# A two-layer decoder trunk: light experts in two matmul passes behind a branch, with weights fetched at register addresses

## The chip, the core and the metric

The kernel runs on one core of one Trainium2 chip, in one launch. The metric is the device time of one execution in microseconds (us), lower is better. The engines are TensorE (PE, its weight loads PEld), VectorE (DVE), ScalarE (ACT), GpSimd (POOL) and SyncE (SP), which here issues the DMAs. Instructions of one engine execute in program order; engines wait for each other through semaphores.

## The reference

A trunk of two layers over 256 tokens of width 1024, float32. Layer 0 is a pooling mixer with sliding-window attention and a dense SwiGLU; layer 1 is a dilated attention with a gated convolution, and then the part that the change is about, a top-2-of-8 expert SwiGLU:

```python
D_MODEL, SEQ, N_EXPERTS, TOP_K, D_FF_EXPERT = 1024, 256, 8, 2, 3584

logits = (xt @ w_router).astype(jnp.float32)
top_logit, top_e = lax.top_k(logits, TOP_K)
gates = jax.nn.softmax(top_logit, axis=-1)
...
    def expert_block(args):
        xb, e = args
        return (jax.nn.silu(xb @ w_gate[e]) * (xb @ w_up[e])) @ w_down[e]
...
x = layer_norm(ALPHA * x + f(x))   # around every sub-layer
```

256 tokens with two experts each are 512 pairs over 8 experts, 64 on average. The weights of the experts are 8 x 3 x 1024 x 3584 float32 numbers.

## The kernel before, in words

**Products in three passes.** Every float32 operand is split into a rounded high part and the low remainder (`split`: ACT casts the high part, DVE subtracts it). A product is then three matmuls into the same PSUM bank (`mm3`, lines 253 to 256): high x high, low x high, high x low. In the experts the tokens are the stationary operand (128 x 128) and the weights are the moving one (128 x 512).

**The weight stream.** All weights lie in DRAM as one stream of pieces of 128 x 2048 floats (1 MB), in the order in which they are used. `Weights` loads them into raw slots with two DMAs each (line 157, issued by SP), `hi` casts the high part (line 200, ACT, tile wh, 4 buffers), `lo` makes the low part (line 216, DVE, tile wl, 3 buffers) and frees the raw slot, and the next load goes into it. `take` hands a piece to the matmuls and `drop` frees its wh and wl and pumps the pieces that follow: wh may be up to three pieces ahead of use and wl up to two. The order of the work is that of the program (a manual schedule).

**The experts.** The router finds for each token and expert a slot in the expert's list (`slot`). The first 128 tokens of an expert are gathered by one-hot matmuls (`Gather`, lines 1094 to 1126), for two experts at a time, 128 columns each, during the last two chunks of the expert before; the gathered high and low parts (xh, xl) have a tile each. An expert is done in 7 chunks of 512 inner columns (loop at line 1213), 6 pieces each. A chunk takes two pieces of gate, two of up (`half_proj`, 16 x 3 = 48 matmuls), then the two pieces of down of the chunk before (`down_half`, 8 x 3 = 24 matmuls). Between them stand Silu on ACT (line 1218), the product on DVE (line 1225), four transposes of h on PE (`flip_h`, line 1136) and the split of the transposed h (lines 127, 128). After an expert's last chunk its output is split and added to the tokens through one-hot matmuls and the gate (`combine`, lines 1165 to 1168).

**The end.** The last chunk's down product is merged in parts. A register with the largest count is then loaded on every engine (line 1305), and a branch (line 1307) enters a loop over all experts only where an expert has more than 128 tokens. That loop addresses its weights by a register. The last layer norm and the stores follow.

Of the kernel before, what the change touches and what calls it, by code (L numbers as in the profile page):

```python
# [37 lines left out]
KEEP, FINE = (8, 20, 16), 10  # L38

C_ID, C_RANK, C_INV, C_END = 0, 128, 136, 168  # L40
# [4 lines left out]
def f32_consts():  # L45
    c = np.zeros((128, C_END), np.float32)
    c[:, C_ID:C_RANK] = np.eye(128)
    c[:, C_INV:C_END] = np.float32(10000.0) ** (-np.arange(32, dtype=np.float32) / np.float32(32))
    c[:, C_RANK:C_INV] = 8 - np.arange(8)
    return c  # L50
# [36 lines left out]
def trunk(ctx, tc, stream, x_tok, x_t, pos, ln_w, ln_b, pool_bd, pool_sc, sinks, conv_w, router, cf, cb, windows,  # L87
# [6 lines left out]
    wsp = ctx.enter_context(tc.tile_pool(name="wsp", bufs=AHEAD + 1))  # L94
    wlp = ctx.enter_context(tc.tile_pool(name="wlp", bufs=AHEAD))
    raw1 = ctx.enter_context(tc.tile_pool(name="raw1", bufs=RAW1))
# [11 lines left out]
    def bank():  # L108
        return ps1.tile([128, 512], F32, name="bank")
# [4 lines left out]
    def acc():  # L114
        return ps2.tile([128, 512], F32, name="acc")
# [13 lines left out]

    class Weights:  # L130
        def __init__(self):
            self.order = list(range(MOE_BASE + 4))
            for s in range(1, NE * NCH):
                self.order += [MOE_BASE + 6 * s + j for j in range(6)]
            self.order += [MOE_BASE + 6 * NE * NCH + j for j in (4, 5)]
            self.raw, self.split, self.owner = {}, {}, {}
            self.free = {(raw1, "raw"): RAW1}
# [5 lines left out]
        def slot(self, dt=F32, last=False):  # L143
            pool = [p for p in self.free if self.free[p]][-1 if last else 0]
            self.free[pool] -= 1
            return pool, pool[0].tile([128, PIECE], dt, name="raw", tag=pool[1])

        def load(self):
            k = len(self.owner)
            self.owner[k], self.raw[k] = self.slot()  # L150
            self.fetch(k, range(2))

        def fetch(self, k, parts, of=2):
            w = PIECE // of
            for q in parts:
                c = slice(q * w, (q + 1) * w)
                nc.sync.dma_start(self.raw[k][:, c], stream[self.order[k]][:, c])

        def top_up(self):
            while len(self.owner) < len(self.order) and sum(self.free.values()) > self.held:  # L160
                self.load()

        def lend(self, tag):
            self.free[big, tag] = 1
            self.top_up()
# [5 lines left out]
        def borrow(self):  # L171
            self.held -= 1
            return self.slot(F32R, True)

        def give_back(self, pool):
            self.free[pool] += 1
            self.top_up()
# [15 lines left out]
        def hi(self, ahead=AHEAD):  # L193
# [3 lines left out]
            if q == 0:  # L197
                self.split[k] = [wsp.tile([128, PIECE], F32R, name="wh"), None]
# [5 lines left out]
        def lo(self):  # L204
# [3 lines left out]
            if q == 0:  # L208
                if k == MOE_BASE - 1:
                    wl = big_tile("xth")  # L210
                else:
                    wl = (ep if k < OUT_BASE and k % 4 == 3 else wlp).tile([128, PIECE], F32R, name="wl")
# [5 lines left out]
            if self.at_lo[0] > k:  # L218
                self.raw.pop(k)
                self.give_back(self.owner[k])  # L220
# [45 lines left out]
    iota = consts.tile([128, B_MASK - B_IOTA], BF16, name="iota")  # L266
# [4 lines left out]
    posi = small.tile([128, 2], I32, name="posi")  # L271
    psc = small.tile([128, 2], F32, name="psc")
# [194 lines left out]
    with tc.tile_pool(name="tmpp", bufs=1, side="right") as tmpp:  # L467
# [13 lines left out]
        for k in range(2):  # L481
            W.owner[k], W.raw[k] = W.slot()
# [481 lines left out]
    raw2 = ctx.enter_context(tc.tile_pool(name="raw2", bufs=RAW2, side="right"))  # L964
# [10 lines left out]
    raw3 = ctx.enter_context(tc.tile_pool(name="raw3", bufs=RAW3))  # L975
    W.free[raw2, "raw"], W.free[raw3, "raw"] = RAW2, RAW3
    W.hold(2)
    mm, na, nb, oa, ob = proj_out(wb, lambda: None)
    ctx.enter_context(tc.manual_schedule())
    held = [W.borrow() for _ in range(2)]  # L980
    xkh, xkl = [t.rearrange("p (i d) -> p i d", i=2) for _, t in held]
# [76 lines left out]
    rank = cst[:, None, C_RANK:C_INV].to_broadcast([128, 2, NE])  # L1058
# [34 lines left out]
    class Gather:  # L1093
        def __init__(self, pool, e0, n, base, tiles):
            self.n, w = n, n * 128
            self.w = w
            self.pool = pool
            self.oh = pool.tile([128, 2, n, 128], F32R, name="oh", bufs=1)
            for i in range(2):
                for e in range(n):  # L1100
                    nc.vector.tensor_scalar(self.oh[:, i, e], iota, slot[:, i, ds(e0 + e, 1)], -float(base),
                                            op0=OP.subtract, op1=OP.is_equal)
            self.xg = [t.rearrange("p (k s) -> p k s", s=w) for t in tiles]

        def half(self, c, a, b, copy):
            w, per = self.w, 512 // self.w
            src = (xkh, xkl)[a]
            for k in range(per):
                for i in range(2):
                    nc.tensor.matmul(b[:, k * w:(k + 1) * w], src[:, i, (c + k) * 128:(c + k + 1) * 128],  # L1110
                                     self.oh[:, i].rearrange("p e s -> p (e s)"), start=i == 0, stop=i == 1)
            copy(self.xg[a][:, c:c + per], b.rearrange("p (k s) -> p k s", s=w))

        def part(self, c):
            self.half(c, 0, bank(), nc.scalar.copy)
            self.half(c, 1, bank(), nc.vector.tensor_copy)

        def back(self):
            n = self.n
            b = bank()  # L1120
            for e in range(n):
                for i in range(2):
                    c = e * 2 + i
                    nc.tensor.transpose(b[:, c * 128:(c + 1) * 128], self.oh[:, i, e].bitcast(F32), identf)
            self.oht = self.pool.tile([128, n, 2, 128], F32R, name="oht", bufs=1)
            nc.scalar.copy(self.oht, b[:, :n * 256].rearrange("p (e i t) -> p e i t", e=n, i=2))
# [6 lines left out]
    def flip_h(pool, h):  # L1133
# [3 lines left out]
        hh = pool.tile([128, 4, 128], F32R, name="hh")  # L1137
        hl = pool.tile([128, 4, 128], F32R, name="hl")
# [3 lines left out]
    def down_half(y, ht, j, n, p):  # L1142
# [26 lines left out]

    ln2.close()  # L1170
    moe = ctx.enter_context(ExitStack())
    m2 = moe.enter_context(tc.tile_pool(name="mo2", bufs=2, side="right"))
    ga = Gather(m2, 0, 2, 0, [big_tile(t) for t in ("mh", "ml")])
    nc.vector.tensor_sub(xkl[:, 1], x[:, 1], xkh[:, 1].bitcast(F32))
    W.lo()
    for c in range(0, KC, 2):
        ga.half(c, 0, acc(), nc.scalar.copy)
    for c in range(0, KC, 2):
        ga.half(c, 1, bank(), nc.vector.tensor_copy if c % 4 == 0 else nc.scalar.copy)
# [3 lines left out]
    most = rt.tile([128, 1], F32, name="most")  # L1183
    nc.vector.tensor_reduce(most, psb[:, 16:24], axis=AX.X, op=OP.max)
    mosti = rt.tile([128, 1], I32, name="mosti")
    nc.vector.tensor_copy(mosti, most)
    gate = small3("gate")

# [8 lines left out]

    def spread(a, h):
# [5 lines left out]
    lent = []  # L1204
    gathers = {0: ga}
    prev = todo = None
    for e, n in [(e, n) for e in range(NE) for n in range(NCH)]:
        xh, xl = [t[:, :, tok(e % 2)] for t in gathers[e // 2].xg]
        gu = []
        for a in range(2):  # L1210
            b = bank()
            for j in range(2):
# [238 lines left out]
```

## Time and profile before

| | |
|---|---|
| time, median of 3 runs | 1467.49 us (1467.12 to 1468.24) |
| span of the profiled execution | 1466.0 us |
| PE busy / weight loads | 1438.0 us (98%) / 1219.7 us (83%) |
| DVE busy | 1174.3 us (80%) |
| ACT busy | 952.1 us (65%) |
| mean granted TensorE clock | 0.995 |
| read from HBM | 424.88 MB, 291 GB/s over the span |
| wl, line 216 (DVE) | 474 instructions, 907.9 us |
| wh, line 200 (ACT) | 476 instructions, 772.1 us |

The span runs from the first to the last instruction of the profiled execution; its time as a run is not given beside it, and the median of the runs is 1.5 us above the span. In the slices of the profile a digit is the busy share in tenths. A row of a group gives the line, the engine, the operation, the tiles (out<-in), the shapes and the count, then busy time and the mean of one, then the idle time before it and what ended it. Matmul durations overlap (their ends are modelled), so the price of one is read from the distance of two starts.

### The profile page before, as it was taken

The page shows a single profiled execution, that of the slowest core. Times are in us where ns is not written, and L with a number is a line of the kernel's source. Part 1 is how long each engine was busy: PE and PEld are TensorE (multiplying, and loading weights), DVE is VectorE, ACT ScalarE, POOL GpSimd, SP SyncE. Part 2 cuts the span into 40 slices and gives each one's busy share as a digit, 9 for nine tenths or more (in the row PEclk, how much of TensorE's full clock was granted, in tenths as well). Part 3 has the DMA queues.
Part 4 walks back from the last instruction along what each step waited for, and adds up shares of the span by engine and source line. Part 5 has one row for each costly group of instructions (what it writes and reads, how often), then busy time and mean ns, then how long its engine had stood idle before and what let it go on. Part 6 is the DMA issues. An engine that isn't in the chain of part 4 may idle for free. (4 is left out here: it accounts for less than half of the span.)

```text
span 1466.0 us, 20100 instructions
## 1 busy us (share of the span) xinstructions
PE 1438.0 (98%) x7665; PEld 1219.7 (83%) x7665; DVE 1174.3 (80%) x1069; ACT 952.1 (65%) x921; POOL 2.5 (0%) x8
## 2 busy tenths in 40 slices
PE   8999999999999999999999999999999999999995
PEld 6889999889997788888888888888888888778884
DVE  6766454686658898988888899898888889889887
ACT  5735444455446777777777777777777777777773
POOL 0000000000000000000000000000000000000000
PEclk9999999999999999999999999999999999999998
DMA  8627655454257999999999999999999899999980
GB/s 260 213 83 233 201 174 190 156 184 162 66 189 299 365 344 363 374 338 311 348 384 355 364 377 346 337 372 410 362 365 341 307 341 369 352 339 340 395 306 31
DMA packets 119323, 426.71 MB, mean 291 GB/s; under 512 B 14130, under 2 KB 14898, under 8 KB 119220
## 3 DMA queue, kind: packets, MB, share of 16 engines
q1 hardware_dynamic: 118356, 424.34, 79.9%
q0 software_dynamic: 576, 0.62, 0.3%
q8 instruction: 62, 1.02, 0.3%
q10 hardware_dynamic: 288, 0.39, 0.1%
q14 instruction: 41, 0.34, 0.1%
HBM read 424.88 MB, written 1.05 MB: 291 GB/s over the span
## 5 line engine op out<-in xcount | busy, mean ns | idle before, releaser
L216 DVE TENSOR_TENSOR wl<-raw,wh 128x2048 fp32r<-128x2048 f32 (+2 forms) x474 | 907.9, 1940 | 97.0 <-ACT wh L200 58.5
L200 ACT CAST wh<-raw 128x2048 fp32r<-128x2048 f32 (+2 forms) x476 | 772.1, 1631 | 159.0 <-PE bank L255 65.2
L254 PE MATMUL acc<-wh,hh 128*128 128x512 f32 (+1 forms) x564 | 221.1, 392 | 0.0
L255 PE MATMUL acc<-wh,hl 128*128 128x512 f32 (+1 forms) x564 | 215.8, 383 | 0.0
L256 PE MATMUL acc<-wl,hh 128*128 128x512 f32 (+1 forms) x564 | 215.6, 382 | 0.0
L254 PE MATMUL bank<-wh,raw 128*128 128x512 f32 x448 | 174.7, 390 | 0.6 <-DVE x L1168 0.6
L254 PE MATMUL bank<-wh,mh 128*128 128x512 f32 x448 | 174.6, 390 | 0.0
L256 PE MATMUL bank<-wl,mh 128*128 128x512 f32 x448 | 174.6, 390 | 0.0
L256 PE MATMUL bank<-wl,raw 128*128 128x512 f32 x448 | 174.6, 390 | 0.0
L255 PE MATMUL bank<-wh,ml 128*128 128x512 f32 x448 | 174.4, 389 | 0.0
L255 PE MATMUL bank<-wh,raw 128*128 128x512 f32 x448 | 174.3, 389 | 0.0
L254 PEld LDWEIGHTS acc<-wh,hh 128*128 128x128 f32 x564 | 105.9, 188 | 22.4 <-issue 3.0
L256 PEld LDWEIGHTS acc<-wl,hh 128*128 128x128 f32 x564 | 105.8, 188 | 22.4
L255 PEld LDWEIGHTS acc<-wh,hl 128*128 128x128 f32 x564 | 106.1, 188 | 19.8 <-DVE hl L128 0.3
L254 PE MATMUL bank<-xth,wh 128*128 128x256 f32 x416 | 118.1, 284 | 0.0
L256 PE MATMUL bank<-xtl,wh 128*128 128x256 f32 x416 | 117.6, 283 | 0.0
L255 PE MATMUL bank<-xth,wl 128*128 128x256 f32 x416 | 117.2, 282 | 0.0
L254 PEld LDWEIGHTS bank<-wh,raw 128*128 128x128 f32 x448 | 84.1, 188 | 18.9 <-DVE x L1168 1.7
L254 PEld LDWEIGHTS bank<-wh,mh 128*128 128x128 f32 x448 | 84.1, 188 | 18.0 <-DVE x L1168 0.6
L256 PEld LDWEIGHTS bank<-wl,raw 128*128 128x128 f32 x448 | 84.1, 188 | 17.7
L256 PEld LDWEIGHTS bank<-wl,mh 128*128 128x128 f32 x448 | 84.1, 188 | 17.6
L255 PEld LDWEIGHTS bank<-wh,ml 128*128 128x128 f32 x448 | 84.1, 188 | 17.3
(246 smaller groups left out, 1668.6 us busy)
## 6 DMA issues: line engine op xcount, KB each, us to landing
raw<-in_stream SPq DMA_DIRECT2D x794, 512.0 KB, 6.7
ln_wb<-in_ln_w SPq DMA_DIRECT2D x3, 512.0 KB, 6.7
ln_wb<-in_ln_b SPq DMA_DIRECT2D x3, 512.0 KB, 10.0
xraw<-in_x_t SPq DMA_DIRECT2D x4, 256.0 KB, 7.4
raw<-in_stream SPq DMA_DIRECT2D x4, 256.0 KB, 6.4
x<-in_x_tok SPq DMA_DIRECT2D x1, 1024.0 KB
win<-in_windows SPq DMA_DIRECT2D x1, 768.0 KB, 11.4
out_dram<-x SPq DMA_DIRECT2D x2, 256.0 KB, 2.0
```

Source lines behind the costliest of these rows:

```text
L200: nc.scalar.copy(self.split[k][0][:, c], self.raw[k][:, c])
L216: nc.vector.tensor_sub(wl[:, c], self.raw[k][:, c], wh[:, c].bitcast(F32))
L254: nc.tensor.matmul(o, ah, bh, start=start, stop=False)
L255: nc.tensor.matmul(o, al, bh, start=False, stop=False)
L256: nc.tensor.matmul(o, ah, bl, start=False, stop=stop)
```

## The change

1. **Sorting on the chip.** After the first chunk of expert 0 the experts 1 to 7 are sorted by their counts on DVE (`sort_experts`). Each engine loads into registers the number of experts 1 to 7 with at most 64 tokens (`nlight`) and the largest count (`nmost`); SP also loads seven addresses into the weight stream.
2. **A branch with two arms.** After the fourth chunk of expert 0, `nlight >= 5` selects an arm. In the first the experts at places 1 to 5 of the sorted order are light and expert 0 and the last two are wide (three passes as before); in the second all are wide. Both contain the rest of the experts and the tail.
3. **Light experts.** The gathered tile has 64 columns of high parts and 64 of low parts side by side as one stationary operand, and a product is two matmuls (with wh and with wl). Rows 0 to 63 and 64 to 127 of the result are added by matmuls with a folding matrix, which also transpose it. The product and the split of h are on 256 columns instead of 512, and Silu too; gate and up are first copied out of PSUM by ACT.
4. **Gathers.** Units are [0], [1, 2], [3, 4], [5], [6], [7] in the first arm, each gathered in 32 matmuls of 128 columns during the last two chunks of the unit before.
5. **Buffers.** Rotating pools become named tiles that are used in turn (`Rings`), so that both arms find them at the same place. Three raw slots become fixed (the tokens' parts and y); the experts' gathers no longer borrow slots.
6. **Smaller moves.** `gates` from the fourth chunk to the first; the load of `nmost` from the end to the third chunk.

```diff
+LIGHT, NLIGHT = 64, 5
+    c[:, C_FOLD:C_INV] = np.arange(128)[:, None] % LIGHT == np.arange(LIGHT)
...
+        def place(self, k, c):
+            if k < MOE_BASE + 4:
+                return stream[self.order[k]][:, c]
+            p, n, j = self.order[k]
+            at = MOE_BASE + 6 * (n + (j >= 4)) + j
+            return stream[ds(self.base[p] + at, 1), :, c] if p else stream[at][:, c]
...
+    W.give_back(*[raw3.tile([128, PIECE], F32, name=f"raw{RAW1 + i}") for i in range(RAW2 + RAW3 - 3)])
...
+    def half_light(b, p, j, xg):
+        for k in range(4):
+            kk = 4 * j + k
+            nc.tensor.matmul(b, xg[:, kk], p[0][:, k], start=kk == 0, stop=False)
+            nc.tensor.matmul(b, xg[:, kk], p[1][:, k], start=False, stop=kk == KC - 1)
+
+    def flip_light(g, u):
+        b = bank()
+        for a, src in enumerate((g, u)):
+            for k in range(4):
+                c = (a * 4 + k) * LIGHT
+                nc.tensor.matmul(b[:, c:c + LIGHT], src[:, k * 128:(k + 1) * 128], fold, start=True, stop=True)
+        h = g[:, :4 * LIGHT]
+        nc.scalar.activation(h, b[:, :4 * LIGHT], AF.Silu)
+        ht = rings.next("hh")
+        s3 = h.rearrange("p (k t) -> p k t", t=LIGHT)
+
+        def rest():
+            nc.vector.tensor_mul(h, h, b[:, 4 * LIGHT:])
+            nc.scalar.copy(ht[:, :, :LIGHT], s3)
+
+        def low():
+            nc.vector.tensor_sub(ht[:, :, LIGHT:], s3, ht[:, :, :LIGHT].bitcast(F32))
+        return (ht,), rest, low
...
-                mm3(o, ht[0][:, c], ht[1][:, c], ph[:, c], pl[:, c], n == 0 and c == 0, n == NCH - 1 and c == 3)
+                start, stop = n == 0 and c == 0, n == NCH - 1 and c == 3
+                if len(ht) == 2:
+                    mm3(o, ht[0][:, c], ht[1][:, c], ph[:, c], pl[:, c], start, stop)
+                else:
+                    nc.tensor.matmul(o, ht[0][:, c], ph[:, c], start=start, stop=False)
+                    nc.tensor.matmul(o, ht[0][:, c], pl[:, c], start=False, stop=stop)
...
+        nc.vector.tensor_scalar(idx, rank, -1.0, 8.0, op0=OP.mult, op1=OP.add)
+        nc.vector.scalar_tensor_tensor(key, cnt, 8.0, idx, op0=OP.mult, op1=OP.add)
+        nc.vector.memset(key[:, 0:1], -1.0)
+        nc.vector.tensor_tensor(grid, cols(key), rows(key), op=OP.is_lt)
+        nc.vector.tensor_reduce(pos, grid, axis=AX.X, op=OP.add)
...
+        nc.vector.tensor_scalar(key[:, 1:], cnt[:, 1:], float(LIGHT), None, op0=OP.is_le)
+        nc.vector.tensor_reduce(outs[:, NE:NE + 1], key[:, 1:], axis=AX.X, op=OP.add)
...
+    for n in range(NCH - 3):
+        first.step(0, n)
+        if n == 0:
+            gates()
+            sort_experts()
+        if n == 2:
+            W.base = [0, *nc.values_load_multi_w_load_instructions(
+                ints[0:1, 1:NE], engines=[mybir.EngineType.SP], min_val=0, max_val=(NE - 1) * PER_EXPERT)[1]]
+            nlight = nc.values_load(ints[0:1, NE:NE + 1], min_val=0, max_val=NE - 1)
+            nmost = nc.values_load(ints[0:1, NE + 1:NE + 2], min_val=0, max_val=T)
+    arms = [[[0], [1, 2], [3, 4], [5], [6], [7]], [[e] for e in range(NE)]]
+    state = W.state()
+    ends = []
+    with tc.If(nlight >= NLIGHT) as cmp:
+        arm = first.copy(arms[0], arms[0][1:4])
+        for s in range(NCH - 3, NE * NCH):
+            arm.step(*divmod(s, NCH))
+        ends.append(tail(arm))
+    W.restore(state)
+    with cmp.Else():
+        arm = first.copy(arms[1], [])
+        for s in range(NCH - 3, NE * NCH):
+            arm.step(*divmod(s, NCH))
+        ends.append(tail(arm))
```

The order of the work in one chunk of a light expert (`Experts.step`): gate's two pieces; the copy of gate (ACT); up's two pieces; the copy of up; the first down piece of the chunk before; the fold (PE) and Silu (ACT); the second down piece; the product (DVE) and the high part of h (ACT). The low part of h (DVE) follows after the next chunk's first piece. In the chunk n == 2 of a light expert its one-hot is built again on DVE (`back`) and transposed on PE.

More of the change, by code (lines that the diff above doesn't have):

```diff
@@ L141, in __init__ @@
             self.at_hi = self.at_lo = (0, 0)
[L143 to L146, printed above, removed]
         def load(self):
-            k = len(self.owner)
-            self.owner[k], self.raw[k] = self.slot()
+            k = self.loaded
+            self.loaded += 1
+            self.raw[k] = self.free.pop(0)
             self.fetch(k, range(2))
@@ L481, in trunk @@
         for k in range(2):
-            W.owner[k], W.raw[k] = W.slot()
+            W.raw[k] = W.free.pop(0)
+        W.loaded = 2
         load_x(0)
@@ L1091, in trunk, with __init__ @@
     nc.vector.tensor_add(slot, off, psb[:, :16].rearrange("p (i e) -> p i e", e=NE))
[L1093 to L1098, printed above, removed]
+    class Unit:
+        def __init__(self, tile, first, n, slots, base=0):
+            self.first, self.n, self.slots, self.base = first, n, slots, base
+            self.wide = n == 0
+            n = max(n, 1)
+            self.oh = rings.next("oh")
+            w = 128 if self.wide else LIGHT
@@ L1112, in half @@
[L1112 to L1119, printed above, removed]
-            b = bank()
[L1121 to L1126, printed above, removed]
+                    nc.tensor.matmul(b[:, k * 128:(k + 1) * 128], src[:, i, (c + k) * 128:(c + k + 1) * 128],
+                                     self.oh[:, i], start=i == 0, stop=i == 1)
@@ L1182, in trunk @@
     W.lo()
[L1183 to L1186, printed above, removed]
     gate = small3("gate")
+    fold = cst[:, C_FOLD:C_INV]
+    slots, gate_of = hots[0], small3("gates")
+    ints = rt.tile([128, NE + 2], I32, name="ints")
     def gates():
@@ L1291, in trunk @@
-    finish(down_half(y, ht, 0, n, W.take(None)))
-    W.drop()
-    split(yh[:, :512], yl[:, :512], y[0])
-    last = down_half(y, ht, 1, n, W.take(None))
-    parts = [slice(512, 768), slice(768, D)]
-    next(last)
-    merge(0, 512)
-    split(yh[:, parts[0]], yl[:, parts[0]], y[1][:, :256])
-    next(last)
-    split(yh[:, parts[1]], yl[:, parts[1]], y[2][:, :256])
-    warm(AF.Sqrt, ht[0][:, 0].bitcast(F32))
-    for m in parts:
-        merge(m.start, 256)
-    nmost = nc.values_load(mosti[0:1, 0:1], min_val=0, max_val=T)
@@ L1314, in trunk @@
+    st, wb = ends[-1]
+    with tc.If(nmost > 128):
+        rings.add("raw", W.free[:2])
+        with tc.For_i(0, NE, 1) as e:
+            ga = Unit(places[1], e, 0, slot, 128)
+            for j in range(4):
+                ga.part(j)
+            ga.back(e)
             y = acc2()
             def get(w, at):
-                raw = raw2.tile([128, PIECE], F32, name="raw", tag="raw")
-                wh = wsp.tile([128, PIECE], F32R, name="wh")
-                wl = wlp.tile([128, PIECE], F32R, name="wl")
+                raw, wh, wl = rings.next("raw"), rings.next("wh"), rings.next("wl")
```

386 lines of the change are left out of this document (241 added, 145 removed).

## The prediction

> **What bounds the kernel now.** I read the page's 40 slices first, then a table of stretches, then the costliest groups between 700 and 1300 us by shape, then the timeline of one chunk of one expert, and last the waits of the DMA queue. In the slices the experts begin in the 13th or 14th, where PE goes to 9 for good and the DMA engines go to 9 with it.
>
> ```profile
> PE   8999999999999999999999999999999999999995
> DVE  6766454686658898988888899898888889889887
> ACT  5735444455446777777777777777777777777773
> DMA  8627655454257999999999999999999899999980
> GB/s 260 213 83 233 201 174 190 156 184 162 66 189 299 365 344 363 374 338 311 348 384 355 364 377 346 337 372 410 362 365 341 307 341 369 352 339 340 395 306 31
> 600.00:620.00 20.00, 20.00 (x91) 16.27 (x90) 19.47 (x14) 13.51 (x10) 0.00 (x0) 1.00 1.00 365
> 980.00:1020.00 40.00, 40.00 (x184) 32.90 (x184) 34.79 (x21) 28.88 (x21) 0.00 (x0) 1.00 1.03 410
> 480.00:600.00 120.00, 120.00 (x543) 98.71 (x542) 105.53 (x65) 91.52 (x62) 0.00 (x0) 1.00 0.99 361
> 723.00:845.00 122.00, 122.00 (x552) 100.20 (x551) 107.56 (x64) 88.68 (x60) 0.00 (x0) 1.00 0.97 363
> ```
>
> The last four rows are stretches: length, then busy time of PE, PEld, DVE, ACT, POOL, then granted clock, DMA share and GB/s. PE is busy without a gap at a full clock: TensorE is the bound. But two others are close. DVE has 107.56 of 122 us (88%), and the DMA engines are in use 97% of the time at 363 GB/s. A third less matmul is therefore not a third less time. The question is how far the period of a chunk can fall before DVE, ACT or the DMA takes over.
>
> ```profile
> L216 DVE TENSOR_TENSOR wl<-raw,wh 128x2048 fp32r<-128x2048 f32 x205 | 462.7, 2286 | 19.9 <-PE bank L256 18.7 <-DMA raw<-in_stream 1.2
> L200 ACT CAST wh<-raw 128x2048 fp32r<-128x2048 f32 x205 | 392.1, 1913 | 63.5 <-PE bank L255 43.3 <-issue 11.3 <-PE acc L255 4.4
> L1225 DVE TENSOR_TENSOR h<-h,bank 128x512 f32<-128x512 f32 x35 | 24.0, 685 | 9.4 <-PE bank L256 9.4
> L127 ACT CAST hh<-bank 128x512 fp32r<-128x512 f32 x34 | 20.0, 588 | 48.4 <-PE bank L1136 48.4
> L1168 DVE SCALAR_TENSOR_TENSOR x<-bank,gate,x 128x512 f32<-128x512 f32 x20 | 13.6, 739 | 0.0
> L788 DVE TENSOR_TENSOR sg<-sg,bank 128x256 f32<-128x256 f32 x20 | 8.4, 421 | 40.7 <-ACT sg L787 40.7
> L787 ACT ACTIVATE sg<-bank 128x256 f32<-128x256 f32 x20 | 7.7, 384 | 59.0 <-PE bank L256 59.0
> L1225 DVE TENSOR_TENSOR h<-h,bank x56: 669/687/690, 478.3 to 1436.3; 128x512 f32<-128x512 f32 x56
> ```
>
> Each chunk (512 of an expert's 3584 inner columns) takes six 1 MB pieces, and each piece costs DVE 2.286 us (wl) and ACT 1.913 us (wh), whatever PE does with it. The last row gives the period: 56 chunks, 958.0 us from the first to the last, 17.42 on average, 121.9 us per expert of seven.
>
> ```profile
> 890.79 0.69 DVE L1225 TENSOR_TENSOR h<-h,bank 128x512 f32<-128x512 f32 x1 [0.38 <-PE bank L256]
> 895.25 6.69 DVE L216 TENSOR_TENSOR wl<-raw,wh 128x2048 fp32r<-128x2048 f32 x3
> 907.69 0.69 DVE L1225 TENSOR_TENSOR h<-h,bank 128x512 f32<-128x512 f32 x1 [0.38 <-PE bank L256]
> 900.00 0.39 PE L254 MATMUL bank<-wh,raw 128*128 128x512 f32 x1
> 902.04 0.39 PE L254 MATMUL bank<-wh,raw 128*128 128x512 f32 x1
> 910.29 0.60 PE L1136 MATMUL bank<-cst,h 128*128 128x128 f32 x4
> 918.94 1.11 PE L1110 MATMUL bank<-oh,raw 128*128 128x256 f32 x8
> 396.48 0.78 PE L947 MATMUL bank<-v,pt 128*128 128x64 f32 x6
> 397.07 0.36 PE L919 MATMUL bank<-kth,qt 128*128 128x256 f32 x1
> L947 PE MATMUL bank<-v,pt 128*128 128x64 f32 x144 | 18.6, 268 | 0.0
> ```
>
> A bare chunk is 907.69 - 890.79 = 16.9 us. Nine matmuls lie between 900.00 and 902.04, so one 512-column matmul costs 0.227 us, and 72 of them with four transposes (0.6) make the 16.9.
>
> **The light chunk.** The input decides first whether it is run. The reference's own router on its inputs gives the experts 72, 72, 59, 63, 55, 73, 57 and 61 tokens. Five of experts 1 to 7 have at most 64, which is just NLIGHT, so experts 1 to 5 of the sorted order run light and three (expert 0 and the last two) stay wide.
>
> PE: 48 matmuls instead of 72 are 10.9 us. The four transposes become eight plain f32 matmuls of 64 columns (fold). L947 has the same shapes: 8 x (3 + 6) = 72 in the code and 144 in the trace, so each is recorded twice, and six records take 397.07 - 396.48 = 0.59 us. Sixteen records are 1.6 us. Together 12.5 us, 4.4 less.
>
> DVE: six wl back to back are 6 x 2.23 = 13.4 us (6.69 for three). The product and the low part of h shrink from 128x512 (0.69) to 128x256 (0.42). Together 14.2 us. Per expert, with the combine (4 x 0.68 = 2.7), the split of y (1.4) and one-hots and gather copies (about 1.2), 7 x 14.2 + 5.3 = 105 us.
>
> ACT: six wh are 11.5; two new evictions of 128x512 before the fold 1.2; Silu and high part on 256 columns 0.8. Together 13.5, and per expert about 97 us.
>
> DMA: 6 x 1.0486 = 6.29 MB. The stretch 980 to 1020 shows 410 GB/s held for 40 us: 15.3 us per chunk, 107.4 per expert. The 361 to 365 of the other stretches is what PE asked for. DVE's wl takes 2.287 us in that stretch (the row below), as elsewhere.
>
> ```profile
> L216 DVE TENSOR_TENSOR wl<-raw,wh 128x2048 fp32r<-128x2048 f32 x15 | 34.0, 2287 | 1.6 <-PE bank L256 1.6
> ACT wh L200 <- PE bank L255: 43.3, 55, 0.8
> ```
>
> So PE falls from first to last, and DVE (105) and the DMA (107.4) are next. The DMA has a credit: up to 11 raw slots, say 8 of them full when the light experts begin, are 8 x 2.56 = 20 us over the five, which makes its share 103. DVE is then the bound at no more than the 97% that it reaches in the stretch 600 to 620 (19.47 of 20). ACT, which executes in order, has 13.5 us of work beside DVE's 14.2, so 0.7 us per chunk is all that it may lose in waiting for PE ahead of the two evictions and Silu. The code lets wh run three pieces ahead of use and wl two, which covers a wait of about one piece. That slack is thin, so I take 96%: 105 / 0.96 = 109 us per light expert. Ends: 105 (DVE with no gap) and 118 (a bare chunk of today, no gain but in what is around it).
>
> A light expert in the middle of today's run costs 7 x 16.9 = 118.3, plus 2.2 for combine and back, 120.5. Five of them: 5 x (120.5 - 109) = **57 us gained**.
>
> **The gathers.** Today three pair gathers stand on PE's path, each four parts of 8 matmuls or 4 x 1.11 = 4.5 us. Afterwards there are five, of which those in expert 0 and in the seventh fall in wide, PE-bound chunks (9 us); the other three lie under DVE in light chunks. **4.5 us gained.**
>
> **What is added.** Rows for the serial parts:
>
> ```profile
> 460.07 0.17 DVE L1070 TENSOR_TENSOR hot<-eq,best 128x16 f32<-128x16 f32 x1
> L1305 DVEq TENSOR_LOAD <-mosti x1: 542/542/542, 1453.0 to 1453.0; - x1
> L1307 DVEq COMPARE_BRANCH  x1: 72/72/72, 1453.7 to 1453.7; - x1
> L1307 PEldq COMPARE_BRANCH  x1: 3892/3892/3892, 1451.2 to 1451.2; - x1
> 1456.63 0.38 DVE ln_mv L365 x2
> L157 SPq DMA_DIRECT2D raw<-in_stream x798: 327/424/1627, 1.2 to 1418.3; - x200
> SPq L157 <- DVE wl L216: 574.4, 250, 9.6
> ```
>
> Sorting is about 21 DVE operations of 0.2 us, with the six of gates moved from the fourth chunk to the first: 5 us ahead of the wl of the second chunk, where DVE is just catching up with PE. Its idle share covers some; I take 2 (0 to 5). Two register loads on each engine, 0.54 us each, in the third chunk: 1 (0 to 1). SP loads nine values; behind it wait only DMA issues, with some 8 pieces (over 20 us of PE's work) loaded ahead: 0, and 4 if the slots were empty. The branch into the first arm should fall through (0.07 us for the compare itself): 1, between 0 and the 5 of an emptied lookahead. At the end each engine jumps over the other arm and then over the overflow loop. Today's one taken branch costs DVE 1456.63 - 1453.7 = 2.9 us before the last norm; a second costs 2.9 more, and the load of nmost (0.54) leaves this place: 2.3 (0.9 to 3.9, the last from PE's row). The copy of cnt, the 32 KB of fold and one raw slot fewer in the out-projection: 1 together. Persistent buffers carry the same dependences as the rotating ones: 0, or 3 either way from a few finer or coarser waits. SP: twelve issues per chunk at 0.424 are 5.1 of 16.9 us, and it mostly waits for DVE; a register address adds register work to each, and 0.5 more would still be hidden. Sum of the added: **7 us lost** (2 to 18).
>
> The Trainium skill's "Runtime: NRT & Kernel Launch", Instruction fetch mechanics, says that a taken branch out of the fetched window stalls for a DMA fetch; the 2.9 us above agree, and no row here tells what a fall-through costs.
>
> **Sum.** 57 + 4.5 - 7 = 54.5 us off the profiled span of 1466.0: 1411.5. The runs' median is 1467.49, 1.5 above that span: **1413**.
>
> **Rivals.**
>
> *The DMA is full already.* For it: a share of 0.97 to 1.00 at 361 to 365 GB/s in most stretches. If 361 is the ceiling, a chunk takes 6.29 / 0.361 = 17.4 us with or without the third pass, nothing is gained, and with the added 7 the time is 1474; at 385 it is 114 per expert before the credit, 110 after it, and the forecast hardly moves. Against it: 410 at a share of 1.03. Chance 0.11, in between more likely than the end: 1440 to 1474.
>
> The Trainium skill's "HBM Reference", Specifications (TRN2), gives an effective 358 GB/s per core, by which a chunk could not go under 17.6 us and the change would gain nothing; it adds that a core streaming alone measures more, about 425. The 40 us at 410 bear out the second, as an estimate 14.8 us per chunk, under DVE's 15.
>
> *ACT and DVE hold each other up.* ACT needs 13.5 of the chunk's 15 and stands in order behind PE twice more than today. If each of the two evictions and Silu costs the 0.8 us of idle that ACT shows before wh today (43.3 us in 55 waits), the thin slack is gone and a chunk takes 16 to 16.5: 1430 to 1450. Chance 0.10.
>
> *The light arm isn't run.* 63 and 61 are near 64, and with one light expert fewer all experts take three passes: seven gathers instead of three (18 us), 7 added, and a taken branch at the start (2.9): 1495, slower. Against it: the counts. Chance 0.05.
>
> *SP becomes the bound: slower.* Place: the twelve register-addressed issues of each chunk after the first four. It decides when one issue costs over 16.9 / 12 = 1.41 us. At the longest of today's issues, 1.63, a chunk takes 19.5 us and 52 chunks lose 2.6 each: about 1600. Against it: 0.424 is the median, and the register work would have to cost twice that again. Chance 0.05.
>
> **How the numbers follow.** Forecast 0.69 (1390 to 1435 by itself), ACT rival 0.10, DMA 0.11, light arm not run 0.05, SP 0.05. Lower end: light experts at 105 with 2 added, 1388. Upper end: into the ACT and DMA rivals, 1450. A change under 0.2% (3 us) can't be told from none here. Faster: 0.69 + 0.10 + 0.08 of the DMA's = 0.87. Same 0.02. Slower: 0.05 + 0.05 + 0.01 = 0.11.
>
> **What would show it.** In the changed profile's five light experts: a period near 15.6 us, DVE at 95% or more, PE near 0.85, 400 GB/s or so, wl still near 2.29 us; L947's doubling seen again in the fold; in the three wide experts 16.9 as before; two taken branches before the last norm. It is wrong if the rate stays at 365 while raw slots stand empty (DMA rival), if ACT's waits for PE in the light stretch are long and DVE's share is under 90% (ACT rival), if SP never waits for DVE, or if 72 matmuls a chunk are still there.

## The result, and the profile after

The changed kernel takes **1399.64 us** (median of 4, 1398.26 to 1401.76) against 1467.75 us for the kernel before beside it: a ratio of 0.954, interval 0.9525 to 0.9552. The forecast was 1413 us with a range of 1388 to 1450; the time lies inside it, 13 us under the point. The profiled execution has a span of 1399.8 us.

Two of the slices' rows of the page after (VectorE's busy tenths, then GB/s):

```profile
DVE  6766555496665889799999999999999998889875
GB/s 259 237 55 222 207 182 193 186 122 209 134 91 232 253 327 362 346 367 399 409 408 409 408 409 409 408 409 408 408 409 404 409 409 404 408 391 261 361 239 34
```

From the 18th slice DVE stands at 9, and from the 20th the DMA engines move 404 to 409 GB/s for 16 slices on end, some 560 us. Stretches (length, then busy time of PE, PEld, DVE, ACT, POOL, then granted clock, DMA share, GB/s): the first two lie in light experts, the third in the wide experts at the end.

```profile
720.00:830.00 110.00, 103.40 (x507) 83.89 (x507) 108.41 (x76) 93.91 (x81) 0.00 (x0) 0.98 1.03 409
830.00:940.00 110.00, 102.46 (x489) 82.49 (x488) 106.62 (x67) 92.97 (x78) 0.00 (x0) 0.97 1.03 409
1134.00:1250.00 116.00, 114.87 (x535) 94.86 (x534) 101.77 (x64) 85.30 (x60) 0.00 (x0) 1.00 1.02 405
```

In the light experts DVE is busy for 97 to 99% of the time. The rows of 600 to 1130 us by shape, for wl and the fold, and the row of the product h on DVE:

```profile
L254 DVE TENSOR_TENSOR wl<-raw,wh 128x2048 fp32r<-128x2048 f32 x211 | 473.1, 2283 | 16.3 <-ACT wh L238 9.7 <-issue 3.6 <-DMA raw<-in_stream 2.7
L1192 PE MATMUL bank<-cst,h 128*128 128x64 f32 x280 | 35.6, 271 | 0.0
```

```profile
L1199 DVE TENSOR_TENSOR h<-h,bank x35: 404/410/423, 609.7 to 1124.6; 128x256 f32<-128x256 f32 x35
```

A wl still costs 2.283 us, and DVE was idle ahead of it for 16 us in 530. The row of h is the period: 35 light chunks, 514.9 us from the first product to the last, 15.14 on average, 106.0 per expert of seven. The waits of SP in 600 to 1130 us (total, times, longest):

```profile
SPq L179 <- DMA raw<-in_stream: 261.2, 349, 1.6
SPq L179 <- DVE wl L254: 37.3, 40, 3.7
```

SP waited almost always for an earlier transfer to land and seldom for DVE to free a slot. One light chunk on DVE's timeline:

```profile
671.51 0.41 DVE L1199 TENSOR_TENSOR h<-h,bank 128x256 f32<-128x256 f32 x1
671.84 2.28 DVE L254 TENSOR_TENSOR wl<-raw,wh 128x2048 fp32r<-128x2048 f32 x1
674.04 0.41 DVE L1203 TENSOR_TENSOR hh<-h,hh 128x256 fp32r<-128x256 f32 x1
674.38 11.09 DVE L254 TENSOR_TENSOR wl<-raw,wh 128x2048 fp32r<-128x2048 f32 x5
685.39 0.41 DVE L1199 TENSOR_TENSOR h<-h,bank 128x256 f32<-128x256 f32 x1
```

685.39 - 671.51 = 13.88 us with nothing between the instructions: six wl and the two halves of h. Three such bare chunks on end, as a stretch:

```profile
657.63:699.27 41.64, 40.11 (x193) 31.69 (x192) 41.64 (x26) 37.88 (x30) 0.00 (x0) 1.00 1.03 410
```

DVE is busy for all of it, and the DMA engines are full as well.

Where the 66.2 us of the span went, from products (`h<-h,bank`) that both kernels have. The row of them all in before stands in the prediction (478.3 to 1436.3); two single ones of before, from DVE's timeline:

```profile
575.61 0.69 DVE L1225 TENSOR_TENSOR h<-h,bank 128x512 f32<-128x512 f32 x1 [0.38 <-PE bank L256]
1207.14 0.69 DVE L1225 TENSOR_TENSOR h<-h,bank 128x512 f32<-128x512 f32 x1 [0.38 <-PE bank L256]
```

And of after, the row of all wide ones, and two from the timeline:

```profile
L1370 DVE TENSOR_TENSOR h<-h,bank x21: 669/687/689, 482.8 to 1365.5; 128x512 f32<-128x512 f32 x21
```

```profile
588.59 0.68 DVE L1370 TENSOR_TENSOR h<-h,bank 128x512 f32<-128x512 f32 x1
1134.67 0.68 DVE L1370 TENSOR_TENSOR h<-h,bank 128x512 f32<-128x512 f32 x1
```

| stretch | before | after | difference | forecast's terms for it |
|---|---|---|---|---|
| start to expert 0's first product | 478.3 | 482.8 | +4.5 | 0 (persistent buffers), small things 1 |
| expert 0, first to seventh product | 97.3 | 105.8 | +8.5 | sort 2, loads 1, branch 1, a gather 4.5 |
| to the first product of the seventh expert (five light ones) | 631.5 | 546.1 | -85.4 | light experts -57, three gathers -13.5 |
| the last two experts | 229.2 | 230.8 | +1.7 | a gather 4.5 |
| last product to the end | 29.7 | 34.3 | +4.6 | two jumps 2.3 |
| sum | 1466.0 | 1399.8 | -66.2 | -54.5 (rounded terms) |

In the light experts the gain was 15 us larger than forecast, and the start, the sort and the end cost more than forecast. The first row is one execution against one: in the ten profiles of this case whose kernels share the changed one's code up to the experts, the first product lands between 480.1 and 484.8 us (median 482.8).

### The profile page after: what moved, and what is told of

Read it like the earlier page. It is cut to its first block, busy times and chain, and to the rows that moved or that the text cites. A ratio compares the mean times of both kernels' runs of the same rounds, so it can differ in the third digit from the quotient of the medians.

```text
span 1399.8 us, 20835 instructions
## 1 busy us (share of the span) xinstructions
PE 1329.3 (95%) x7309; PEld 1124.5 (80%) x7309; DVE 1147.9 (82%) x1093; ACT 963.9 (69%) x1001; POOL 2.5 (0%) x8
## 5 line engine op out<-in xcount | busy, mean ns | idle before, releaser
L1185 PE MATMUL bank<-wl,ml 128*128 128x512 f32 x336 | 133.6, 398 | 4.0 <-DVE wl L254 4.0
L1228 PE MATMUL acc<-wh,hh 128*128 128x512 f32 x280 | 116.9, 417 | 0.0
L1229 PE MATMUL acc<-wl,hh 128*128 128x512 f32 x280 | 115.1, 411 | 1.6 <-DVE wl L254 0.4
L291 PE MATMUL acc<-wh,hh 128*128 128x512 f32 (+1 forms) x284 | 107.7, 380 | 0.0
L292 PE MATMUL acc<-wh,hl 128*128 128x512 f32 (+1 forms) x284 | 105.0, 370 | 0.6 <-DVE hl L130 0.6
L293 PE MATMUL acc<-wl,hh 128*128 128x512 f32 (+1 forms) x284 | 105.0, 370 | 0.0
L1184 PE MATMUL bank<-wh,mh 128*128 128x512 f32 x224 | 89.7, 401 | 0.3
L291 PE MATMUL bank<-wh,mh 128*128 128x512 f32 x224 | 88.3, 394 | 0.8 <-DVE x L1245 0.8
L292 PE MATMUL bank<-wh,mh 128*128 128x512 f32 x224 | 87.8, 392 | 0.0
L291 PEld LDWEIGHTS bank<-xth,wh 128*128 128x128 f32 x416 | 79.8, 192 | 0.4
L292 PEld LDWEIGHTS bank<-xth,wl 128*128 128x128 f32 x416 | 79.8, 192 | 0.4
L293 PEld LDWEIGHTS bank<-xtl,wh 128*128 128x128 f32 x416 | 79.8, 192 | 0.0
## 6 DMA issues: line engine op xcount, KB each, us to landing
raw<-in_stream SPq DMA_DIRECT2D x794, 512.0 KB, 10.1
```

The lines of the kernel that those rows point to most:

```text
L291: nc.tensor.matmul(o, ah, bh, start=start, stop=False)
L292: nc.tensor.matmul(o, al, bh, start=False, stop=False)
L293: nc.tensor.matmul(o, ah, bl, start=False, stop=stop)
L1184: nc.tensor.matmul(b, xg[:, kk], p[0][:, k], start=kk == 0, stop=False)
L1185: nc.tensor.matmul(b, xg[:, kk], p[1][:, k], start=False, stop=kk == KC - 1)
L1228: nc.tensor.matmul(o, ht[0][:, c], ph[:, c], start=start, stop=False)
```

## Experiments: what sets the light expert

**A third pass again.** In light experts the matmul with wl is issued twice, in `half_light` and in `down_half`.

```diff
             nc.tensor.matmul(b, xg[:, kk], p[0][:, k], start=kk == 0, stop=False)
+            nc.tensor.matmul(b, xg[:, kk], p[1][:, k], start=False, stop=False)
             nc.tensor.matmul(b, xg[:, kk], p[1][:, k], start=False, stop=kk == KC - 1)
```

> In the light experts each product with wl is issued twice, so that a chunk has 72 matmuls again beside the fold (the low part counts double in the output). Theory (the third pass was what bound the chunk): PE needs 72 x 0.227 + 1.6 = 17.9 us per chunk, a light expert takes about 129 us instead of 105, and the time is about 1520 us. Rival (the gain came from the buffers, the order of the experts or earlier loads, and the pass was hidden anyway): within 10 us of 1400.

Measured: **1532.15 us** in one run, 132.5 more than the changed kernel. Two products of neighbouring chunks and a stretch of its light experts:

```profile
949.25 0.42 DVE L1200 TENSOR_TENSOR h<-h,bank 128x256 f32<-128x256 f32 x1
967.40 0.42 DVE L1200 TENSOR_TENSOR h<-h,bank 128x256 f32<-128x256 f32 x1
```

```profile
720.00:830.00 110.00, 110.00 (x539) 92.36 (x538) 88.75 (x59) 76.70 (x64) 0.00 (x0) 1.00 0.94 341
```

PE is the bound again, and a bare chunk takes 18.15 us, more than the 16.9 of a wide one; the fold, at 1.6 us dearer than the transposes at 0.6, is most of the difference. Without the 24 extra matmuls (0.227 each) the light chunk would be 12.7 us of PE. The gain of the change is thus the skipped pass, and a bare chunk stopped at 13.88 instead of 12.7.

**All experts wide.** The light arm needs eight light experts of seven and is never entered. The expectation below says that the branch stays; the trace says otherwise. The branch's line, 1462, has two instructions on each of five engines in the changed kernel's trace and none on any engine here. The register is declared to hold at most seven, so the condition was probably settled when the kernel was built; that is not shown. So this run has neither the entry nor a jump over the other arm.

```diff
-LIGHT, NLIGHT = 64, 5
+LIGHT, NLIGHT = 64, 8
```

> NLIGHT is 8, so the branch takes the second arm and every expert has three passes; sorting, register addresses, persistent buffers and the branch stay. Theory (these parts only cost): the time before plus four more gathers (18 us) plus what the trace of the changed kernel shows as lost at the start (4.5), at the sort (4.8) and at the end (4.6), plus a taken branch (3): about 1503 us. Rival (the buffers or the addresses give part of the gain): 1470 us or less.

Measured: **1487.9 us** in one run, span 1486.1, 20.1 above the span before; between forecast and rival. The products run from 484.7 to 1456.0:

```profile
L1370 DVE TENSOR_TENSOR h<-h,bank x56: 667/687/689, 484.7 to 1456.0; 128x512 f32<-128x512 f32 x56
```

So 6.4 us lie ahead of the first product, 13.3 between the first and the last, 0.4 behind. Of the 13.3 the sort takes 4.8 (below). The 8.5 left are put down to seven gathers one by one in place of three for two, about half of the 18 that the forecast's rival took; they were not timed singly. The end costs nothing here, where one jump stands ahead of the last norm as before the change. The light arm, with its branch and its second jump, is worth 88 us.

**VectorE or the DMA freed, and then both.** In light experts the low parts are made for half of the columns; or half of each piece is loaded; or both. The matmuls read the other half from what the buffers held. Each kernel ran once.

```diff
+    def of_light(at):
+        return isinstance(at, tuple) and 1 <= at[0] <= 5
...
-            self.fetch(k, range(2))
+            self.fetch(k, range(1 if of_light(self.order[k]) else 2))
...
+            if of_light(self.order[k]):
+                c = slice(0, PIECE // 2)
```

> In the light experts DVE makes wl for half of each piece's columns only (the other half keeps older numbers). Theory (DVE binds the light chunk, and the DMA at its 409 GB/s stands just behind it): the DMA then binds, 210 pieces x 2.564 us less some 8 that are loaded ahead are 518 us against 523 now, so 1393 to 1400 us. Rival A (DVE alone binds, the DMA has room): down to ACT's 97 us per expert, about 1362 us. Rival B (ACT and PE hold each other up): no change, 1400 us.

> In the light experts only half of each piece is loaded (the other half keeps older numbers); DVE, ACT and PE do all their work. Theory (DVE binds): DVE has its 103 to 104 us per expert still, so 1393 to 1400 us, with the DMA share near a half in this stretch. Rival A of the run before (DVE alone): the same. Rival C (the DMA binds and DVE only waits for it): DVE's share of the stretch falls well under 97% now and the time falls by more than 10 us.

> In the five light experts half of each weight piece is loaded and the low parts are made for half of the columns (the matmuls read the rest from what the buffers held before). Freeing VectorE alone gave 0 us and freeing the DMA engines alone 5 us. Theory (the two tie, each keeps the time when the other is freed): with both freed the next limit is TensorE, whose light chunk was reckoned at 12.5 us and was seen at 12.7 us while the DMA engines still had loaded buffers in hand; so the light experts fall from 104.7 to about 100 to 102 us each, and the time to 1374 to 1388 us. Rival (the engines hold each other up through the order of the work, whatever the load): no better than the DMA-freed kernel, 1392 us or more. A second rival: VectorE and the DMA engines alone set it, and TensorE is far from its limit: below 1365 us.

Measured: half the low parts **1399.52 us**, half the loads **1394.36 us**, both **1361.12 us**. One stretch and the period of each, in this order (and two neighbouring products of the last):

```profile
720.00:830.00 110.00, 101.21 (x500) 83.59 (x499) 63.12 (x73) 94.79 (x81) 0.00 (x0) 0.98 1.03 409
```

```profile
L1204 DVE TENSOR_TENSOR h<-h,bank x35: 410/414/423, 609.1 to 1121.2; 128x256 f32<-128x256 f32 x35
```

```profile
720.00:830.00 110.00, 103.55 (x501) 84.11 (x500) 106.91 (x72) 93.08 (x81) 0.00 (x0) 0.97 0.61 203
```

```profile
L1202 DVE TENSOR_TENSOR h<-h,bank x35: 407/413/421, 607.3 to 1118.0; 128x256 f32<-128x256 f32 x35
```

```profile
720.00:830.00 110.00, 106.26 (x532) 89.18 (x531) 68.72 (x78) 100.55 (x89) 0.00 (x0) 0.98 0.69 222
```

```profile
L1204 DVE TENSOR_TENSOR h<-h,bank x35: 410/416/423, 611.0 to 1083.1; 128x256 f32<-128x256 f32 x35
```

```profile
746.33 0.41 DVE L1204 TENSOR_TENSOR h<-h,bank 128x256 f32<-128x256 f32 x1
759.05 0.41 DVE L1204 TENSOR_TENSOR h<-h,bank 128x256 f32<-128x256 f32 x1
```

With DVE at 57% the 35 chunks still take 512.1 us (514.9 before the edit; 513.8 to 515.3 in the profiles of the six other kernels here that leave the light chunk as it is), now at the 409 GB/s of the DMA. With the DMA at 61% they take 510.7, now on DVE alone (97%). With both freed they take 472.1. The two limits stand within 1% of each other, and either one alone keeps the time. The 409 GB/s move 34 chunks of 6.29 MB in 523 us; 512 is possible because loaded slots were drained meanwhile. The kernel with half the low parts shows it: three bare chunks of its first light expert, then three of its third:

```profile
649.85:688.00 38.15, 38.15 (x194) 32.41 (x192) 24.06 (x26) 37.44 (x31) 0.00 (x0) 1.00 1.03 409
855.04:901.73 46.69, 42.36 (x194) 34.80 (x193) 24.06 (x26) 38.97 (x31) 0.00 (x0) 0.93 1.03 409
```

The first three take 12.7 us each, from slots that were full; the later three take 15.4 to 16.0, and 6.29 MB at 409 GB/s are 15.4. With both freed a bare chunk takes 759.05 - 746.33 = 12.72 us, the same as PE's 12.7 worked out from the third pass. Three of them there:

```profile
651.76:689.89 38.13, 38.13 (x193) 32.40 (x192) 24.07 (x26) 37.42 (x31) 0.00 (x0) 1.00 0.74 247
```

TensorE is the next limit, 1.2 us below today's bare chunk. ScalarE is busy for 37.42 of the same 38.13 us (98%), so it stands right behind: fewer matmuls alone could take at most 0.2 us more off a bare chunk. The expectation's theory had the mechanism, but its 100 to 102 us per expert were reckoned badly: seven chunks of 12.7 are 89, and with combine and gathers 97 was measured. The second rival named the right time for the wrong reason, since PE is busy without a gap in the bare chunks there. That the engines hold each other up through their order is refuted: the same order of work goes through 43 us faster.

## Experiments: what the change added

**The persistent buffers alone.** The kernel before, with wh, wl and the single raw slots as named tiles in turn, and nothing else.

```diff
-    wsp = ctx.enter_context(tc.tile_pool(name="wsp", bufs=AHEAD + 1))
+    wsp = ctx.enter_context(tc.tile_pool(name="wsp", bufs=1))
...
-                self.split[k] = [wsp.tile([128, PIECE], F32R, name="wh"), None]
+                self.split[k] = [turn_of("wh"), None]
```

> The kernel before, with only one part of the change: the high-part, low-part and single raw weight buffers are made once and handed out in turn, in place of pools that rotate. The three passes, the order of the experts and the end stay as before. Theory (the 4.5 us by which the first expert starts later after the change come from the persistent buffers): the first expert's first product lands 4 to 6 us later than 478.3 us, and the time is 1471 to 1474 us. Rival (the delay is from another part of the change): within 0.2% of before, 1467 to 1469 us, with the first product at 478 us.

Measured: **1471.61 us** against 1468.78 (medians of 10 and 13), ratio 1.0019 (1.0008 to 1.0031), 2.8 us more. The first product lands at 482.8 us as after the change, and from there to the last product it is 958.0 us as before:

```profile
L1237 DVE TENSOR_TENSOR h<-h,bank x56: 669/687/690, 482.8 to 1440.8; 128x512 f32<-128x512 f32 x56
```

The largest single step is near 322 us in layer 1. PE's one wait between 310 and 335 us in the kernel before, and ACT's weight casts between the first copy of v (at 315.13 us) and the cast that PE waits for:

```profile
PE bank L320 <- ACT kth L322: 0.4, 1, 0.4
```

```profile
317.13 1.05 ACT L200 CAST wh<-raw 128x1024 fp32r<-128x1024 f32 x1 [1.75 <-DMA raw<-in_stream]
318.33 1.05 ACT L200 CAST wh<-raw 128x1024 fp32r<-128x1024 f32 x1
320.76 1.05 ACT L200 CAST wh<-raw 128x1024 fp32r<-128x1024 f32 x1 [1.38 <-DMA raw<-in_stream]
321.73 0.36 ACT L322 CAST kth<-bank 128x256 fp32r<-128x256 f32 x1
```

The same with persistent buffers (the copy of v is at 316.05):

```profile
PE bank L332 <- ACT kth L334: 2.4, 1, 2.4
```

```profile
318.23 1.05 ACT L212 CAST wh<-raw 128x1024 fp32r<-128x1024 f32 x1 [1.91 <-DMA raw<-in_stream]
320.05 1.05 ACT L212 CAST wh<-raw 128x1024 fp32r<-128x1024 f32 x1 [0.77 <-DMA raw<-in_stream]
322.45 1.05 ACT L212 CAST wh<-raw 128x1024 fp32r<-128x1024 f32 x1 [1.15 <-PE bank L318]
324.05 1.04 ACT L212 CAST wh<-raw 128x1024 fp32r<-128x1024 f32 x1 [0.56 <-DMA raw<-in_stream]
325.00 0.36 ACT L334 CAST kth<-bank 128x256 fp32r<-128x256 f32 x1
```

The dependences are the same, but in this attention the order of ACT's instructions is not written out by hand, and with other buffers it came out otherwise: four weight casts in place of three stand ahead of the key's cast (kth), three of them wait for their transfers, and the key waits behind them. The Trainium skill's "PSUM — Partial Sum Buffer", Engine vs sequencer instructions, calls ScalarE's queue strictly first in, first out; PE's wait of 2.4 us in place of 0.4 is what that costs here. Where the rest of the 4.5 us between the two profiles lies was not traced.

**The sort later.** The order is worked out after the second chunk of expert 0; the gates themselves, which the change had moved to the first chunk, and the sorted places and gates follow after the fourth.

```diff
-        if n == 0:
+        if n == 1:
+            place = sort_experts()
+        if n == 3:
             gates()
-            sort_experts()
+            place(slot, slots)
+            place(gate, gate_of)
```

> The changed kernel with the gates and the sort moved: the order is worked out after the second chunk of expert 0, and the sorted places and gates after the fourth, in place of all of it after the first chunk. Theory (the 4.8 us by which the first chunk's interval grew is VectorE work on the path, and VectorE has room later in the TensorE-bound expert): about 4 us less than the changed kernel, 1394.5 to 1397.5 us. Rival (the sort only moves the same work to a place where it delays as much): 1399 to 1401 us.

**One jump at the end.** The loop for experts of more than 128 tokens stands in the wide arm alone (the light arm asks also that no expert has more), and the last norm and the stores stand in each arm.

```diff
+        nc.vector.tensor_scalar(key[:, 0:1], outs[:, NE + 1:], 128.0, None, op0=OP.is_le)
+        nc.vector.tensor_mul(outs[:, NE:NE + 1], outs[:, NE:NE + 1], key[:, 0:1])
...
-        ends.append(tail(arm))
+        close(*tail(arm))
```

> The changed kernel with one taken jump at its end in place of two: the loop for experts of more than 128 tokens stands only in the wide arm (the light arm is then entered only if no expert has more than 128), and the last normalization and the stores stand inside each arm. Theory (the two jumps, 2.9 and 4.3 us on VectorE ahead of the last normalization, are on the path): the span from the last expert's last product to the end falls from 34.3 to 27 to 30 us, the time to 1393 to 1396 us. Rival (the jump's cost returns behind the stores, where the program has to end all the same): 1398 to 1400 us.

Measured: **1400.15 us** and **1400.56 us**, ratios of 0.9542 (0.9522 to 0.9563) and 0.9529 (0.9504 to 0.9554), no gain that four runs each can show. Their profiles show one. After the change DVE's 21 operations of the sort stood in a row from 486.32, right behind the six of the gates (the first and the last of them, of the changed kernel, then the second product); with both later the second product follows 12.36 us after the first, as before the change, instead of 17.2. From the first to the seventh product that kernel takes 101.4 us in place of 105.8:

```profile
486.32 0.16 DVE L1296 TENSOR_SCALAR u<-cst 128x8 f32<-128x8 f32 x1
490.55 0.22 DVE L1312 TENSOR_REDUCE gates<-u 128x8 f32<-128x64 f32 x1
499.98 0.69 DVE L1370 TENSOR_TENSOR h<-h,bank 128x512 f32<-128x512 f32 x1 [0.40 <-PE bank L293]
```

```profile
480.33 0.69 DVE L1372 TENSOR_TENSOR h<-h,bank 128x512 f32<-128x512 f32 x1 [0.16 <-PE bank L293]
492.69 0.69 DVE L1372 TENSOR_TENSOR h<-h,bank 128x512 f32<-128x512 f32 x1 [0.37 <-PE bank L293]
```

The jumps on DVE at the end of the changed kernel, and the norm behind them; two branches at line 1462 are the entry at 537.8 and the jump over the other arm at 1383.4:

```profile
L1462 DVEq COMPARE_BRANCH  x2: 51/53/55, 537.8 to 1383.4; - x2
L1475 DVEq COMPARE_BRANCH  x1: 69/69/69, 1386.2 to 1386.2; - x1
L1475 DVEq EVENT_SEMAPHORE  x1: 21/21/21, 1390.5 to 1390.5; - x1
```

```profile
1390.64 0.39 DVE L402 BATCH_NORM_AGGREGATE ln_mv<-raw 128x2 f32<-128x24 f32 x2 [6.68 <-DVEq L1475]
```

The first jump takes 2.8 us, the second 4.3, and DVE is idle for 6.68 us against 3.07 before the change. With one jump left the span from the last product to the end was 31.1 us instead of 34.3, less of a gain than the 27 to 30 forecast. The start of the norm and the last work of DVE in that kernel:

```profile
1385.80 0.39 DVE L1465 BATCH_NORM_AGGREGATE raw<-raw 128x2 f32<-128x24 f32 x2
1390.19 1.54 DVE L1477 SCALAR_TENSOR_TENSOR x<-x,raw,raw 128x512 f32<-128x512 f32 x3
```

Here the norm starts 18.4 us after the last product (1367.4), in the changed kernel 25.1 us after it. But from DVE's last work to the end of the span it is 6.8 us in place of 3.2: the jump that is left now stands there (SP's at 1392.1, behind the last store that it issues), and 3.5 of the 6.7 us come back. So the expectation's rival was right by half. The four runs of the late sort spread over 10.4 us and those with one jump over 6.6, more than either saving.

**Together, and with the early order restored.** Four kernels beside each other: the changed one again; both edits; rotating pools up to the experts, whose buffers the experts then take over; and all three edits.

```diff
+    def turn_of(name):
+        if name in rings.at:
+            return rings.next(name)
+        t = (wsp if name == "wh" else wlp).tile([128, PIECE], F32R, name=name)
+        turns[name] = [*turns[name], t][-AHEAD - (name == "wh"):]
+        return t
...
+    for name in turns:
+        rings.add(name, turns[name])
```

> The changed kernel itself, unchanged, as the measure for the three kernels beside it on the same chip: 1398 to 1402 us.

> The changed kernel with both of the edits timed singly before: the sort split and moved behind the second and fourth chunks of expert 0, and the overflow loop, the last normalization and the stores inside the arms, so that one taken jump is left at the end. Theory (the profiles of the single edits showed 4.3 us saved between the first expert's first product and the light experts, and 3.2 us saved behind the last product, and both are on the path; their medians hid it because the start of the first expert moves by some us from run to run): 5 to 8 us less than the changed kernel beside it, 1392 to 1395 us. Rival (what is saved there is given back elsewhere, as the single medians say): within 2 us of it.

> The changed kernel with rotating pools for the high parts, low parts and single raw buffers up to the experts, as before the change; the buffers that are then in hand are taken over in turn by the experts. Up to the experts ScalarE's instructions then stand in the order of the kernel before. Theory (the persistent buffers let one more weight cast stand ahead of the key's cast in ScalarE's queue, and cost 2.8 us in the kernel before): the first expert's first product lands at 478 to 479 us in place of 482.8 us, and the time is 2 to 5 us below the changed kernel beside it. Rival (the delay is no matter of the order): 482 to 485 us, and the time within 2 us.

> All three edits together: early rotating pools, the sort split and moved, one jump at the end. Theory (three separate costs of the change, each on the path): 8 to 12 us less than the changed kernel beside it, 1388 to 1392 us. Rival (only the early order counts): 1395 to 1398 us.

| kernel | median of 5, us | lowest to highest | ratio to before |
|---|---|---|---|
| changed, again | 1402.40 | 1398.21 to 1406.41 | 0.9552 (0.9530 to 0.9573) |
| sort later, one jump | 1396.09 | 1393.49 to 1400.43 | 0.9511 (0.9491 to 0.9530) |
| early rotating pools | 1398.44 | 1396.86 to 1399.48 | 0.9521 (0.9507 to 0.9535) |
| all three | **1391.10** | 1390.71 to 1391.64 | 0.9473 (0.9460 to 0.9486) |

By the medians, sort and jump save 6.3 us without and 7.3 us with the early pools; the pools save 4.0 and 5.0. The 7.3 and the 5.0 stand clear: no run of one kernel reaches into the other's range. The 6.3 and the 4.0 do not, as the ranges overlap; against all nine runs of the changed kernel in this case (median 1400.3) they are 4.2 and 1.9. Beside the changed kernel the three differences of 4.0, 6.3 and 11.3 lie where the theory put them (2 to 5, 5 to 8, 8 to 12); as a time, the 1396.09 lies 1 us above the 1392 to 1395 expected. The last kernel beats both that the case began with. With rotating pools three weight casts stand ahead of the key's cast as before, and PE's wait for the key is back at 0.3 us (0.7 with all three edits, 1.4 to 3.2 in the eleven profiles with persistent buffers):

```profile
PE bank L371 <- ACT kth L373: 0.3, 1, 0.3
```

The first product lands at 479.2 us with the early pools alone and at 481.8 with all three edits, which lies within what persistent buffers gave (480.1 to 484.8), so a single profile of the start does not settle it; the medians do.

## Why the prediction was right, and where its terms were off

- **The order of the limits held.** PE falls from first to last, DVE is next, the DMA just behind it: DVE at 97 to 99%, 409 GB/s, wl at 2.283 us, the fold doubled in the records (two groups of 280 for 35 x 8 matmuls; one is shown above), wide chunks about 17 us. PE's light chunk was put at 12.5 us and measured 12.7.
- **The light expert was mis-sized: 109 us forecast, 106.0 measured.** Two parts of the term were a little off. The divisor 0.96 for ACT, DVE and PE waiting for each other was too low: DVE was busy for 0.977 of the two light stretches, and 105 over 0.977 is 107.5. And DVE's work was 103.6 (0.977 of 106.0), not 105: a bare chunk takes 13.88 us and not 14.2, as five wl back to back stand 2.20 us apart (11.01 for five) and not 2.23. Five times 3 us are the 15 by which the stretch of light experts beat its terms (-85.4 against -70.5).
- **The DMA's ceiling was right, its role too small.** 409 GB/s against 410 taken from 40 us of before. The forecast put it, with the credit of loaded slots, at 103 us per expert, 6 under DVE's 109; the two were within 1%, 105.4 with DVE freed and 105.1 with the DMA freed. The credit of 8 pieces or 20 us was too large: 512.1 us in place of 523 are 11, some 4 pieces. The Trainium skill's "HBM Reference", Specifications (TRN2), has 358 GB/s as a core's effective share and about 425 for a core alone; this core, the only one that the kernel uses, held 409, so the first would have been 12% too low a ceiling.
- **The added 7 us were 13 to 14 in this profile.** The persistent buffers were put at 0 or 3 either way for the waits' sake; they cost 2.8 us in the kernel before and up to 5 in the changed one, at least 2 of it through the order of ACT's queue, which the forecast did not consider. The sort was put at 2 of 0 to 5 and took 4.8. The second jump was put at the first one's 2.9 and took 4.3; the end lost 4.6, above the upper bound of 3.9.
- **Some agreement is luck.** For expert 0 the forecast's terms add up to the measured 8.5, but the sort took more than its 2, and the loads and the branch showed nothing of their 1 each. For the whole, the start and the end lost 3.5 and 2.3 us more than forecast and the last two experts 2.8 less, so that some 12 of the 15 us are left.
- **The branch's entry was put at 1 and costs nothing that the rows show:** expert 0's chunks around it have the same intervals with the branch falling through as in the kernel with all experts wide, which has no branch there (16.78 and 17.77 us in both). No run here shows an entry that is taken.
- **The rivals** fell: the rate did not stay at 361, light experts were run, SP waited for landings and not with its own work, and ACT's order cost little (DVE waited 9.7 us in 530 for wh).
- **One sign was wrong:** PE at 0.85 was to show in the light stretch, and it reads 0.94. In part the busy share of a PE that is kept waiting reads too high: in three bare chunks it reads 40.11 of 41.64 us, 0.96, where the same matmuls took 38.13 us with both limits freed, 0.92.

## What to carry to other kernels

Before a pass is taken from the engine that bounds, work out the period of each of the others from their own rows and the best rate that any stretch shows; here that gave 105, 107 and 106.0 was reached, and halving one of two tied limits brought next to nothing. Where a change needs buffers at fixed places, see that the order of the stages before it stays as it was, for instance by taking over the buffers that the rotating pools leave. Of the time added by sorting and branching, most was in serial places: put small VectorE work where another engine bounds, and end each arm on its own, which gave back 3.2 of the 4.6 us at the end.

## What was not expected of the hardware

- One core held 404 to 409 GB/s for some 560 us from one DMA queue, while SP waited for landings; over the whole kernel the median from issue to landing rose from 6.7 us to 10.1 us (512 KB each).
- Two taken jumps in a row cost DVE 2.8 and 4.3 us, while a branch that fell through in mid-work cost nothing visible. What the second jump has that the first has not was not tried.
- The changed kernel's runs spread over 8 us (1398.2 to 1406.4), with the early order restored over 2.6, and with all three edits over 0.9. That the casts that wait for transfers make the spread is likely, but was not shown.
